# Sums of y squared as rows: nine columns with one column of ones as the weights, and the squares moving

## The chip, the cores and the metric

One core of one Trainium2 chip. The metric is device time in microseconds (us) of one execution of the program; lower is better. TensorE (PE in the rows; its weight loads PEld), VectorE (DVE), ScalarE (ACT), GpSimd (POOL) and SyncE (SP, which issues the DMAs) run side by side and wait for one another by semaphores.

## The reference

One layer of a hybrid decoder step: a feed-forward half step, a mixer of two heads side by side (S5 and SSD), a second half step, a last norm. All is f32; 1024 prompt positions and 8 x 4 sample positions, 1056 in all. What matters here is the end of the SSD head: `y` is divided by the root of its mean square over the 384 channels of its group, for each position and each of four groups.

```python
ys = (ys + ssd_d.astype(f32)[:, None] * xh).reshape(b, l, SSD_WIDTH) * jax.nn.silu(z)
yg = ys.reshape(b, l, SSD_GROUPS, SSD_WIDTH // SSD_GROUPS)
yg = yg * lax.rsqrt(jnp.mean(yg * yg, axis=-1, keepdims=True) + EPS)
o_ssd = yg.reshape(b, l, SSD_WIDTH) * ssd_norm.astype(f32)
out = jnp.concatenate([o5, o_ssd], axis=-1).astype(h.dtype) @ w_out
```

## The kernel before

Channels lie on partitions, positions in the free dimension. Each large product is done in three matmuls of a high and a low part (L317 to L319 in `dense`: weights 128x128, three blocks of 352 positions, four PSUM banks in turn in the mixer). These matmuls are the clock of the program: after each unit of three, `tick` counts one, and other work is put between units. There are two queues of such steps (`later`: a step runs so many ticks after the one before it in its queue), and `at` for a step at a set tick. The order of instructions on each engine is the order in which they are written out this way; nothing reorders them later.

While the projections of SSD group g + 1 run in `dense` (`group`: eight tiles of 24 units each), the chunked scan of group g runs in queue 0 (`ssd_steps`; its sequence is in `steps`). The 1056 positions are nine chunks: c = 0 to 7 of 128 positions, and c = 8, the 32 sample positions, which is done first. For each chunk, `stage_a` makes the decays and transposes (L1744 to L1747), `stage_b` multiplies (L1801 with 64 weight columns, two halves of the array at once; L1802 with 128) and `y_done` makes `y`, its squares over the three channel tiles, and on GpSimd their sum over the three in `ysq` (128 channels x positions). `y_sums` sums `ysq` over its 128 partitions: one f32 matmul (L1787) with `ysq` as the weights and one column of ones moving, which gives one column with positions on partitions, and a VectorE step L1788 (in the rows L152, the helper `ts`) that scales it into column c of `rv` [128, 9]. It is called with the next chunk's `stage_b`, behind L1802, or alone: for c = 6 and c = 8 in `sample_done`, for c = 7 in the tail. In the trace an f32 matmul is two instructions, so the 36 sums are 72.

The last steps of a group are its tail, three steps that run at the start of the next group's sequence, 4, 10 and 5 ticks apart: `stage_b(7)`; the last sum and `rs_root` (a square root on ScalarE, then a reciprocal and eight steps of Newton's method on VectorE, all on [128, 9], L392 to L397); and `rs_row` (L399 to L405): a transpose on TensorE to [9, 128], a VectorE copy of it into `rr`, and the store of that to `rsd[2 + g]` in DRAM. For group 3 the tail runs under the output projection (`mix_out`). From `rsd` it is loaded back, spread over 128 partitions (`rs_load`, L409), when the output projection of the group is prepared (`begin`, `ahead`). `rs_col`, `rs_root` and `rs_row` also serve the three norms over the 1024 channels (`rs_steps`), which the change leaves as they are: of the seven transposes L403, four are the tails'.

`tmp()` hands out three SBUF slices in turn, `abank()` the side banks of PSUM in turn.

Of the kernel before, what the change touches and what calls it, by code (L numbers as in the profile page):

```python
# [31 lines left out]
EPS = 1e-6  # L32
RND = 12582912.0
ADD, SUB, MUL = ALU.add, ALU.subtract, ALU.mult
# [100 lines left out]
class Build:  # L135
# [249 lines left out]
        self.ts(v[0:32, 8:9], ps[0:32, 8:9], 1.0 / n, MUL, EPS, ADD)  # L385
        yield from self.rs_root(y)

    def rs_root(self, y):
        nc, v, t = self.nc, self.rv, self.rt
        self.act(t, v, AF.Sqrt)  # L390
        yield 2
        nc.vector.reciprocal(y, t)  # L392
        for _ in range(2):
            self.tt(t, y, y, MUL)
            self.tt(t, t, v, MUL)
            self.ts(t, t, -0.5, MUL, 1.5, ADD)
            self.tt(y, y, t, MUL)  # L397
# [1287 lines left out]
    def ssd_tiles(self, S):  # L1685
        f = lambda name, *s: S.tile([128, *s], F32, name=name)
        self.abc = f("abc", 6, 128)
        self.ysq = f("ysq", 128)
        self.xb = Slots(S, 3, [128, 5, 128], F32, "xb")
        self.zg = Slots(S, 2, [128, 3, 128], F32, "zg")  # L1690
        self.prod = deque((f(f"dec{i}", 6, 128), f(f"ce{i}", 6, 128), f(f"xd{i}", 384), f(f"xds{i}", 384), f(f"bt{i}", 128))
                          for i in range(2))
        self.hT, self.hS, self.yf = f("hT", 384), f("hS", 384), f("yf", 3, 128)
        self.h0 = Slots(S, 3, [128, 384], F32, "h0")
        self.ces, self.ys, self.xs, self.zs = f("ces", 6, 32), f("ys", 3, 32), f("xsm", 3, 32), f("zsm", 3, 32)
        self.bst = S.tile([96, 128], F32R, name="bst")
        self.bm = [S.tile([96, 128], F32R, name=f"bm{i}") for i in range(2)]
        self.xst = S.tile([96, 384], F32R, name="xst")
        self.tail, self.rs_done = [], set()

    def ssd_steps(self, g):
        nc, L, o = self.nc, self.later, self.o
# [15 lines left out]
        def load_z(c):  # L1718
            n = 32 if c == 8 else 128
            z = self.zs if c == 8 else self.zg.get()  # L1720
            nc.sync.dma_start(z, self.dZ[g, :, :, 128 * c:128 * c + n].rearrange("j p c -> p j c"))
            cur["z", c] = z
# [48 lines left out]
        def y_done(c, n, x, z, p3, s):  # L1771
            cs = slice(128 * c, 128 * c + n)
            y = self.yf[:, :, 0:n]
            for j in range(3):
                self.stt(y[:, j], x[:, j], self.dcol[:, 3 * g + j:3 * g + j + 1], p3[:, j], MUL, ADD)
            self.tt(y, y, z, MUL)
            self.act(s, y, AF.Square)
            self.store(self.dO[g, :, :, cs].rearrange("j p c -> p j c"), y)
            self.tt(s[:, 0], s[:, 0], s[:, 1], ADD, nc.gpsimd)
            self.tt(self.ysq[:, 0:n], s[:, 0], s[:, 2], ADD, nc.gpsimd)  # L1780
            cur["sum"] = (c, n, self.ysq[:, 0:n])

        def y_sums(p):

            if "sum" in cur:
                c, n, s = cur.pop("sum")
                nc.tensor.matmul(p[0:n, 400:401], s, self.ones[:, 0:1], start=True, stop=True)  # L1787
                return lambda: self.ts(self.rv[0:n, c:c + 1], p[0:n, 400:401], 1.0 / 384, MUL, EPS, ADD)  # L1788
            return lambda: None

        def stage_b(c):
            xb, (dec, ce, xd, xds, bt) = cur.pop(c)
            z = cur.pop(("z", c))
            p3, p4 = self.abank(), self.abank()
            for j in range(3):
                for off in range(2 if c else 1):
                    for e in range(2):
                        out = p3[64 * e:64 * e + 64, 128 * j:128 * j + 128]
                        r = 2 * j + e
                        lhs, rhs = ((xd, dec), (self.hT, ce))[off]  # L1800
                        nc.tensor.matmul(out, lhs[:, 64 * r:64 * r + 64], rhs[:, r], start=(off == 0), stop=(off == 1 or c == 0))  # L1801
            nc.tensor.matmul(p4[:, 0:384], bt, xds, start=True, stop=True)  # L1802
            done = y_sums(p3)
            yield GAP["b_pe"]
            done()
            if c == 0:
                nc.vector.tensor_copy(self.hT, p4[:, 0:384])
            else:
                self.tt(self.hT, self.hS, p4[:, 0:384], ADD)
            if c < 7:  # L1810
                self.tt(v6(self.hS), v6(self.hT), self.cd[:, c + 1, h6, None].broadcast_to([128, 6, 64]), MUL, nc.gpsimd)
            yield GAP["b_y"]
            y_done(c, 128, xb[:, 2:5], z, p3[:, 0:384].rearrange("p (j c) -> p j c", j=3), xd.rearrange("p (j c) -> p j c", j=3))
            self.xb.put(xb)
            self.zg.put(z)
            if c == 7:
                nc.sync.dma_start(o["ssdp"][g], self.hT)

        def sample_load(b):
            h0 = self.h0.get()  # L1820
            nc.sync.dma_start(h0, self.a["h0"][g, :, b])
            cur["h", b] = h0
# [9 lines left out]
        def sample_m(b):  # L1832
            self.ts(self.bm[b % 2], self.bst.bitcast(F32), self.bmask[:, b:b + 1], MUL)

        def sample_out(b):
            h0 = cur.pop(("h", b))
            nc.sync.dma_start(o["ssds"][g, :, b], h0)
            self.h0.put(h0)

        def sample_h(b):  # L1840
            h0, bm, p = cur["h", b], self.bm[b % 2], self.abank()
            if b:
                sample_out(b - 1)
            if b + 2 < 8:
                self.at(GAP["sample"], lambda: sample_load(b + 2))
            for r in range(6):
                out = p[64 * (r % 2):64 * (r % 2) + 64, 384 + 4 * (r // 2):388 + 4 * (r // 2)]
                nc.tensor.matmul(out, h0[:, 64 * r:64 * r + 64], self.ces[:, r, 4 * b:4 * b + 4], start=True, stop=True)
            nc.tensor.matmul(p[:, 0:384], bm, self.xst, start=True, stop=True)
            self.tt(v6(h0), v6(h0), self.cds[:, b, h6, None].broadcast_to([128, 6, 64]), MUL, nc.gpsimd)  # L1850

            def add():
                y = self.ys[:, :, 4 * b:4 * b + 4]
                self.tt(y, y, p[:, 384:396].rearrange("p (j c) -> p j c", j=3), ADD)
                self.tt(h0, h0, p[:, 0:384], ADD)
                if b < 7:
                    sample_m(b + 1)

            self.at(GAP["add"], add)

        def sample_done():
            y_sums(self.abank())()
            sample_out(7)
            y_done(8, 32, self.xs, self.zs, self.ys, self.xs)
            nc.vector.memset(self.rv[:, 8:9], 1.0)
            yield GAP["done4" if g == 3 else "done2"]
            y_sums(self.abank())()

# [6 lines left out]
        def steps(nxt=None):  # L1875

            tail, self.tail = self.tail, [
                lambda: stage_b(7),
                lambda: (y_sums(self.abank())(), self.rs_root(self.ry))[1],
                lambda: (self.rs_row(self.ry, self.rsd[2 + g]), self.rs_done.add(g)),  # L1880
            ]
            ga, gb, gh = (GAP[k + ("3" if g == 3 else "")] for k in "abh")
            for i in range(9):
                c = (i + 8) % 9
                L((GAP["first"], GAP["second"])[i] if i < 2 else ga, lambda c=c: stage_a(c))
                if i == 0:
                    for n, fn in enumerate(tail):
                        L(GAP[f"tail{n}"], fn)
                    L(0, lambda: (load_z(8), load_z(0), sample_load(0), sample_load(1), sample_m(0)))
                else:  # L1890
                    L(gb, sample_b if i == 1 else lambda c=c: stage_b(c - 1))
                    if c < 7:
                        L(0, lambda c=c: self.at(6, lambda: load_z(c + 1)))
                    L(gh, lambda b=i - 1: sample_h(b))
            if nxt:
                L(0, nxt)
            L(GAP["done3" if g == 3 else "done"], sample_done)
# [250 lines left out]
```

## Time and profile before

| | |
|---|---|
| median of 3 runs | 2311.99 us (2311.85 to 2312.82) |
| profiled execution | 2316.52 us, of which the span of its instructions is 2314.8 us |
| busy in the span | TensorE 98%, VectorE 65%, ScalarE 37%, GpSimd 16% |
| mean granted TensorE clock | 0.993 |

A row of the time order gives the start in us from the span's start, the duration, engine, line, operation, output<-inputs, the shape of the weights (rows*columns) and the moving operand, the count of merged instructions, and in brackets the idle time ahead of it. A matmul's duration holds its latency; how fast they follow one another is read from the starts. A list of waits gives the total in us, the count and the longest one.

### The profile page before, as it was taken

Reading aid. Unit: us, or ns where it says so; the run is one execution under the profiler, and the core shown is the slowest. Engines: PE = TensorE matmul, PEld = TensorE weight load, DVE = VectorE, ACT = ScalarE, POOL = GpSimd, SP = SyncE. Lnnn points to the kernel's source line nnn. Section 1 sums busy time; section 2 is a strip of 40 time slices with the busy share of each in tenths; the row PEclk is TensorE's granted clock in tenths of the full one; section 3 lists DMA queues with packets and bytes.
Section 4 is the critical chain, followed back from the end, with each engine's and each line's share of the span. In section 5 each row is a group of like instructions: output and inputs, shape, how many; then the busy total and the mean of one; then the engine's idle time right before and its main releaser. Section 6 shows DMA issues by size and latency. Waiting matters only on the chain. (4 is left out here: it accounts for less than half of the span.)

```text
span 2314.8 us, 40918 instructions
## 1 busy us (share of the span) xinstructions
PE 2274.9 (98%) x16463; PEld 2218.2 (96%) x16463; DVE 1503.8 (65%) x3110; ACT 845.0 (37%) x1373; POOL 363.8 (16%) x425
## 2 busy tenths in 40 slices
PE   9999999999999999999999999999999999999997
PEld 9999999999999899999999889999999999999997
DVE  5988887662326377787889778867855555552325
ACT  5433344440113133455555563233433333331122
POOL 1200000000002133242333434422100000000013
PEclk9999999999999999999999999999999999999999
DMA  4222233362311354563555645432222122263112
GB/s 149 82 68 92 102 118 104 120 227 99 102 54 45 115 189 144 157 189 125 174 159 167 213 126 158 141 127 84 88 79 78 71 84 83 88 243 119 62 48 75
DMA packets 191549, 274.68 MB, mean 119 GB/s; under 512 B 31616, under 2 KB 137343, under 8 KB 191359
## 3 DMA queue, kind: packets, MB, share of 16 engines
q1 hardware_dynamic: 190782, 271.54, 35.8%
q8 instruction: 129, 2.11, 0.4%
q14 instruction: 62, 0.50, 0.1%
q10 hardware_dynamic: 576, 0.52, 0.1%
HBM read 195.17 MB, written 76.84 MB: 118 GB/s over the span
## 5 line engine op out<-in xcount | busy, mean ns | idle before, releaser
L317 PE MATMUL b<-xn,ws 128*128 128x352 f32 (+3 forms) x1776 | 589.7, 332 | 2.9 <-DVE x L145 2.2
L318 PE MATMUL b<-xn,ws 128*128 128x352 f32 (+3 forms) x1776 | 575.0, 324 | 2.4 <-DVE xn L155 2.4
L319 PE MATMUL b<-xn,ws 128*128 128x352 f32 (+3 forms) x1776 | 574.4, 323 | 0.0
L317 PEld LDWEIGHTS b<-xn,ws 128*128 128x128 f32 x1776 | 335.7, 189 | 9.4 <-DVE x L145 3.5
L681 PE MATMUL b<-xn,ws 128*128 128x264 f32 x1184 | 338.3, 286 | 5.4 <-ACT g L158 5.4
L318 PEld LDWEIGHTS b<-xn,ws 128*128 128x128 f32 x1776 | 337.5, 190 | 4.0 <-DVE xn L155 3.0
L683 PE MATMUL b<-xn,ws 128*128 128x264 f32 x1184 | 337.5, 285 | 2.3 <-DVE ws L145 2.3
L682 PE MATMUL b<-xn,ws 128*128 128x264 f32 x1184 | 338.3, 286 | 0.0
L319 PEld LDWEIGHTS b<-xn,ws 128*128 128x128 f32 x1776 | 335.8, 189 | 0.0
L158 ACT ACTIVATE ws<-wr 128x512 fp32r<-128x512 f32 (+4 forms) x208 | 170.4, 822 | 328.7 <-PE b L318 271.8
L145 DVE TENSOR_TENSOR ws<-wr,ws 128x512 fp32r<-128x512 f32 (+4 forms) x208 | 220.3, 1060 | 81.5 <-ACT ws L158 81.0
L681 PE MATMUL b<-d,ws 128*128 128x264 f32 x888 | 253.6, 286 | 1.0 <-DVE g L145 0.8
L682 PE MATMUL b<-d,ws 128*128 128x264 f32 x888 | 253.4, 285 | 0.0
L683 PE MATMUL b<-d,ws 128*128 128x264 f32 x888 | 252.3, 284 | 0.0
L155 DVE SCALAR_TENSOR_TENSOR x<-b,x 128x352 f32<-128x352 f32 (+2 forms) x144 | 73.4, 522 | 246.4 <-PE b L319 246.3
L681 PEld LDWEIGHTS b<-xn,ws 128*128 128x128 f32 x1184 | 223.3, 189 | 7.3 <-ACT g L158 6.7
L145 DVE TENSOR_TENSOR g<-b,g 128x264 f32<-128x264 f32 (+1 forms) x311 | 134.2, 433 | 147.5 <-PE b L683 104.5
L683 PEld LDWEIGHTS b<-xn,ws 128*128 128x128 f32 x1184 | 223.8, 189 | 3.1 <-DVE ws L145 3.1
L145 POOL TENSOR_TENSOR acc<-acc,g 128x400 f32<-128x400 f32 (+2 forms) x25 | 37.6, 1505 | 1195.8 <-ACT g L158 1195.6
L682 PEld LDWEIGHTS b<-xn,ws 128*128 128x128 f32 x1184 | 223.2, 189 | 0.0
L317 PE MATMUL b<-d,ws 128*128 128x352 f32 (+2 forms) x534 | 172.7, 323 | 0.0
L319 PE MATMUL b<-d,ws 128*128 128x352 f32 (+2 forms) x534 | 172.1, 322 | 0.0
(344 smaller groups left out, 4255.8 us busy)
## 6 DMA issues: line engine op xcount, KB each, us to landing
wr<-in_gu SPq DMA_DIRECT2D x68, 512.0 KB
dH<-g SPq DMA_DIRECT2D x74, 264.0 KB
wr<-in_win SPq DMA_DIRECT2D x36, 512.0 KB
wr<-in_dn SPq DMA_DIRECT2D x32, 512.0 KB
d<-dH SPq DMA_DIRECT2D x24, 528.0 KB
abc<-dA SPq DMA_DIRECT2D x32, 384.0 KB
xn<-dH SPq DMA_DIRECT2D x20, 528.0 KB
dC<-acc SPq DMA_DIRECT2D x20, 528.0 KB
```

Source lines behind the costliest of these rows:

```text
L145: (eng or self.nc.vector).tensor_tensor(out, x, y, op=op)
L155: self.nc.vector.scalar_tensor_tensor(out, x, s, y, op0=op0, op1=op1)
L158: self.nc.scalar.activation(out, x, f, **k)
L317: nc.tensor.matmul(p, wh[:, kc], xh, start=(k == 0), stop=False)
L318: nc.tensor.matmul(p, wh[:, kc], xl, start=False, stop=False)
L319: nc.tensor.matmul(p, wl[:, kc], xh, start=False, stop=(k == K - 1))
L681: nc.tensor.matmul(q, wh, xh, start=(k == 0 and name in ("P1", "P2", "P5")), stop=False, skip_group_check=True)
L682: nc.tensor.matmul(q, wh, xl, start=False, stop=False, skip_group_check=True)
L683: nc.tensor.matmul(q, wl, xh, start=False, stop=(k == 3), skip_group_check=True)
```

## The change

The sum's operands change places. The weights are nine columns [128, 9] cut from a new tile `hot` of 17 columns, all zeros but the middle one, so that the ones stand in column c of the nine; `ysq` moves. The result has the sums of chunk c in row c of [9, 128] and zeros in the other rows, and VectorE adds it onto `yr` (which is the old `rr` [9, 128]). When all nine are in, `y_root` scales, takes the root as before but on [9, 128], and stores the result itself; the transpose, its copy and the third step of the tail go. The result lies in a slice of `tmp()`, the scratch in `ysq`, and `yr` is cleared for the next group.

```diff
-    def rs_root(self, y):
-        nc, v, t = self.nc, self.rv, self.rt
+    def rs_root(self, y, v=None, t=None):
+        nc, v, t = self.nc, self.rv if v is None else v, self.rt if t is None else t
...
+        self.hot, self.yr = f("hot", 17), self.rr
+        self.nc.vector.memset(self.hot, 0.0)
+        self.nc.vector.memset(self.hot[:, 8:9], 1.0)
+        self.nc.vector.memset(self.yr, 0.0)
...
                 c, n, s = cur.pop("sum")
-                nc.tensor.matmul(p[0:n, 400:401], s, self.ones[:, 0:1], start=True, stop=True)
-                return lambda: self.ts(self.rv[0:n, c:c + 1], p[0:n, 400:401], 1.0 / 384, MUL, EPS, ADD)
+                q = p[0:9, 384:384 + n]
+                nc.tensor.matmul(q, self.hot[:, 8 - c:17 - c], s, start=True, stop=True)
+                return lambda: self.tt(self.yr[:, 0:n], self.yr[:, 0:n], q, ADD)
...
+        def y_root():
+            y_sums(self.abank())()
+            self.ts(self.yr, self.yr, 1.0 / 384, MUL, EPS, ADD)
+            y = self.tmp()[0:9, 0:128]
+            yield from self.rs_root(y, self.yr, self.ysq[0:9])
+            nc.sync.dma_start(self.rsd[2 + g], y)
+            nc.vector.memset(self.yr, 0.0)
...
             y_done(8, 32, self.xs, self.zs, self.ys, self.xs)
-            nc.vector.memset(self.rv[:, 8:9], 1.0)
...
                 lambda: stage_b(7),
-                lambda: (y_sums(self.abank())(), self.rs_root(self.ry))[1],
-                lambda: (self.rs_row(self.ry, self.rsd[2 + g]), self.rs_done.add(g)),
+                y_root,
+                lambda: self.rs_done.add(g),
```

## Rows read from the trace of the kernel before

**Rows 1.** The page, busy time by engine: us, share of the span, instructions.

```profile
PE 2274.9 (98%) x16463; PEld 2218.2 (96%) x16463; DVE 1503.8 (65%) x3110; ACT 845.0 (37%) x1373; POOL 363.8 (16%) x425
```

**Rows 2.** Stretch 940 to 1515: length, busy PE, PEld, DVE, ACT, POOL; clock, DMA.

```profile
940.00:1515.00 575.00, 567.08 (x4212) 533.42 (x4212) 470.82 (x1075) 285.02 (x406) 208.97 (x252) 0.99 0.52 160
```

**Rows 3.** TensorE's waits from 940 to 1620, the two longest groups: total, times, longest.

```profile
PE b L1787 <- POOL ysq L145: 4.2, 2, 3.2
PE b L318 <- DVE xn L155: 2.4, 2, 1.7
```

**Rows 4.** TensorE in order of time: an old sum over 128 positions.

```profile
1064.56 0.32 PE L318 MATMUL b<-xn,ws 128*128 128x352 f32 x1
1064.72 0.32 PE L319 MATMUL b<-xn,ws 128*128 128x352 f32 x1
1064.88 0.28 PE L1787 MATMUL b<-ones,ysq 128*128 128x1 f32 x2
...
1065.27 0.33 PE L318 MATMUL b<-xn,ws 128*128 128x352 f32 x1
```

**Rows 5.** The same view: an f32 matmul with 128 weight and 128 moving columns.

```profile
1094.62 0.38 PE L1744 MATMUL b<-xb 128*128 128x128 f32 x2
1094.83 0.27 PE L1745 MATMUL b<-ident,xb 128*128 128x128 f32 x1
```

**Rows 6.** The same view: the old sum over the 32 sample positions.

```profile
1067.83 0.32 PE L319 MATMUL b<-xn,ws 128*128 128x352 f32 x1
1068.09 0.22 PE L1787 MATMUL b<-ones,ysq 128*32 128x1 f32 x2
1068.24 0.43 PE L317 MATMUL b<-xn,ws 128*128 128x352 f32 x1
1068.51 0.32 PE L318 MATMUL b<-xn,ws 128*128 128x352 f32 x1
```

**Rows 7.** The same view, earlier: into an f32 matmul with 16 weight columns.

```profile
309.69 0.28 PE L682 MATMUL b<-xn,ws 128*128 128x264 f32 x1
309.81 0.28 PE L683 MATMUL b<-xn,ws 128*128 128x264 f32 x1
310.02 0.63 PE L1216 MATMUL b<-x,x 64*16 64x128 f32 x16
```

**Rows 8.** The same view: from 64 weight columns to 128, in a chunk's second stage.

```profile
981.97 0.39 PE L1801 MATMUL b<-ce,hT 128*64 128x128 f32 x4
982.29 0.91 PE L1802 MATMUL b<-xds,bt 128*128 128x384 f32 x2
983.04 0.28 PE L1787 MATMUL b<-ones,ysq 128*128 128x1 f32 x2
```

**Rows 9.** Line L403, weight loads: ns min/median/max, first and last start.

```profile
L403 PEld LDWEIGHTS b<-ident,ry x7: 87/87/133, 46.8 to 1594.6; 128*9 128x9 f32 x7
```

**Rows 10.** TensorE in order of time: transposes in group 0's and group 3's tail.

```profile
1089.79 0.32 PE L319 MATMUL b<-xn,ws 128*128 128x352 f32 x1
1090.18 0.27 PE L403 MATMUL b<-ident,ry 128*9 128x128 f32 x1
...
1090.45 0.32 PE L318 MATMUL b<-xn,ws 128*128 128x352 f32 x1
...
1510.99 0.32 PE L319 MATMUL b<-xn,ws 128*128 128x352 f32 x1
1511.78 0.28 PE L403 MATMUL b<-ident,ry 128*9 128x128 f32 x1 [0.46 <-DVE ry L145]
...
1512.05 0.32 PE L318 MATMUL b<-xn,ws 128*128 128x352 f32 x1
```

**Rows 11.** VectorE groups from 940 to 1515: busy us, mean ns, idle before.

```profile
L152 DVE TENSOR_SCALAR rv<-b 128x1 f32<-128x1 f32 x32 | 4.8, 150 | 1.2 <-PE b L1787 1.1
L145 DVE TENSOR_TENSOR rt<-rt,rv 128x9 f32<-128x9 f32 x8 | 1.4, 171 | 0.3
L404 DVE COPY rr<-b 9x128 f32<-9x128 f32 x4 | 1.1, 276 | 0.5 <-PE b L403 0.5
```

## The prediction

> **What bounds the kernel now.** I read the busy times of the page first. TensorE is busy for 98% of the span, so the reader is to see that whatever lengthens TensorE's stream lengthens the kernel, unless it falls into one of the few places where TensorE waits [rows 1]. The next view is the table of one stretch, from 940 to 1515 us, in which all of the changed code runs: TensorE 567.1 of 575.0 us, VectorE 470.8, the others far less [rows 2]. VectorE has 104 us to spare there, TensorE 8. The third view is the list of TensorE's waits around that stretch: the longest are two waits of the old sums themselves for GpSimd's `ysq`, 4.2 us together, and two for VectorE's `xn`, 2.4 us [rows 3]. All else was read from the order of TensorE's instructions in time, where what counts is the distance between starts, since matmuls are pipelined and a matmul's own duration holds its latency. Undisturbed, two matmuls of 352 columns start 0.16 us apart [rows 4].
>
> **What the change does to TensorE: the sums.** There are 36 of them, nine in each of four groups: eight over 128 positions (c = 0 to 7) and one over 32 (c = 8). Each is one f32 matmul, which the trace shows as two instructions. Before, the squares are the weights (128 columns of them) and one column of ones moves. From the start of the L319 ahead to the start of the L318 behind it takes 0.55 us instead of 2 x 0.16, so an old sum of 128 costs 0.23 us [rows 4]: that is two weight loads, since the moving column is next to nothing. After, the weights are the nine columns cut from `hot`, and the squares move, 128 columns. What 128 moving f32 columns cost is in the L1744 rows: its two instructions take from 1094.62 to 1094.83, 0.105 each, 0.21 together [rows 5]. By that alone old and new would be equal, 0.23 and 0.22.
>
> What decides is another thing in the rows: an f32 matmul whose weights have few columns doesn't run in a stream with the full ones. The old sum of c = 8 has 32 weight columns and one moving column. The L319 ahead of it is followed after 0.26 us instead of 0.16, and from that L319 to the L318 behind it takes 0.68 us, so it costs 0.36 us although it moves and loads less than the old sum of 128 [rows 6]. The pause at the entry, 0.10, stands also before L1216, with 16 weight columns: 0.21 from the L683 ahead, where 0.12 is the rule [rows 7]. At the exit a pause stands behind L1801, whose weights have 64 columns: its last four start 0.32 us ahead of L1802, where their work is 0.22 (two halves at once, so twice the 0.105), and the two full ones of 384 columns that follow take 0.75 where three times 0.21 is 0.63 [rows 5, 8]: 0.10 + 0.12. So the new sum of 128, between full matmuls, is estimated as 0.10 of entry, 0.21 of moving, 0.02 for a first load that wasn't fetched ahead, and 0.22 of exit: 0.55 us. The other way round, the old sum of c = 8, 0.36, plus 0.21 for the columns moved, less some 0.05 for its own two short instructions (0.15 from the first of them to the L317 behind, the exit's 0.10 included), gives 0.52 [rows 6]. I take 0.54, so 0.31 more for each of 32 sums: 9.9 us. The four sums of 32 positions moved one column and now move 32; both pay the pauses; a quarter of 0.21 is 0.05, of which a part is covered: +0.03 each, 0.1 together.
>
> Is nine columns like 16, 32 and 64, or like 128? The nearest row by width speaks for 128: L403, a transpose, has nine weight columns too, loaded in 87 ns [rows 9], and its group 0 row, 1089.79 to 1090.45, has only the L403's own time and a wait in it [rows 10]; in other transposes no entry pause is to be seen. But L403 is a transpose, and L1787 at 32 and L1216 at 16 are plain f32 matmuls as the new one is. I take the nearest in kind. [...]
>
> **TensorE: the transposes.** Four of the seven L403 go. In the last group it is 1510.99 to 1512.05, 1.06 us against 0.32, so 0.74, of which 0.46 is waiting for VectorE's last step of the root; in the first group 0.66 against 0.32, so 0.34 [rows 10]; the two between them, read in the same way, 0.23 and 0.12. Gain: 1.4 us. No wait takes their place on TensorE, since nothing on it reads the root any more; the root's row goes from VectorE straight to the store, and the load of it that the next stage needs stands behind that.
>
> **The other engines.** VectorE: 32 evictions of one column, 150 ns, become adds of 9x128 out of PSUM, which the copy of L404 stands for, 276 ns [rows 11]: with the four small ones 36 x 0.13 = 4.7 us. The root's operations go from 128x9, 171 ns, to 9x128; taken as the same 276 ns, the nine of a root are 0.95 us more, and with the scaling and the clearing that are new, less the copy L404, about 1.1; 4.4 in all [rows 11]. These 9 us lie in VectorE's 104 us of idle time [rows 2]; ten operations of the root stand in one row ahead of evictions, but four PSUM banks turn in the dense loop and each is filled for 24 matmuls, 3.8 us, so a delay of 1 us is covered. If that cover is gone, they are paid in full (a rival below). Three clearing operations at the opening of the pool, under 0.3 us each by the copy's row, stand on VectorE ahead of the first eviction of group 1; `hot` lies where the S5 stage's `un0` was, which was last read by slice 5 of 8, so they wait for nothing recent. ScalarE: one square root of 128 elements for one of nine, four times, off the path. The store of the root moves from the third step of the tail to the second, ahead of what SP issues in those 5 ticks: loads of z and h stood behind it before as well; stores of `acc` can now wait for the end of the root, some 1 us, and are next needed a whole tile (24 units of three matmuls, 11.5 us) later. GpSimd's next write of `ysq` must wait for the root that uses it as scratch, and comes a whole chunk later. The ring of `tmp` turns once more and the ring of side banks once less per group; both have had their readers finished by then. All these I cost at nothing.
>
> **The sum.** 9.9 + 0.1 - 1.4 = 8.6 us. Two of the new sums wait for `ysq` anyway [rows 3], and there the entry pause is hidden: -0.2. So +8.4 us on the profiled execution's 2316.5 us (2314.8 of span and 1.7 around it). Its time is 0.2% over the median of the runs shown, 2312.0, and the stretch is TensorE's in both, so I add it to the median: 2320.4 us. With the spread of the single terms (0.29 to 0.33 for a sum, 1 us for the rest) the case has 2318 to 2323.
>
> **Rivals.** (A) Nine columns run as full ones do, and the nine-column load is cheap: then a new sum is the 0.21 of moving with a little of the next load, against 0.23, and a sum of 32 falls from 0.36 to about 0.15. 32 x -0.01, 4 x -0.2 and -1.4 make -2.5: 2309.5 us, no slower. It decides if a new sum costs under 0.4 us. For it speaks L403, against it L1787 at 32 and L1216. 12%. [...] The trace speaks against it for f32, with 0.105 for each instruction [rows 5]; I leave it 2 of the 12.
>
> (B) The time is absorbed: the 4.2 us for which the sums wait for GpSimd [rows 3] could shrink by as much as TensorE comes later. That takes up to 4.2 us off: 2316. Against it: the work that GpSimd is late with hangs on VectorE and ScalarE steps that are issued by TensorE's own count of units, so it moves along. 8%, 2313 to 2317.
>
> (C) VectorE's 9 us bite: the adds and the roots stand ahead of evictions and of the `xn` that TensorE waits for, or a clearing waits for the old owner of its place. If a third to a half of the 9 us comes through, 2323 to 2326. For it: VectorE is the second busiest, 82% of the stretch [rows 2]; against it, the longest of TensorE's waits for it are two with 2.4 us together [rows 3]. 14%.
>
> **How the numbers follow.** Forecast 66%, A 12, B 8, C 14. The predicted time is the forecast's, 2320.4. The range reaches through B and C, 2313 to 2326, and leaves out A and the far ends. A measurement of this kernel can tell some 0.2%, 4.6 us, from no change: faster than 2307.4 is only the end of A, 3%; between that and 2316.6 lie the rest of A, most of B and a strip of the forecast, 17%; slower 80%.
>
> **What the profile after would show.** Right: behind each L1802 a gap of 0.1 us before the sum; weight loads of nine columns that start with their matmul and not one matmul ahead; 0.5 to 0.55 us from the last full matmul to the next full stream; only three L403; the span longer in the 940 to 1515 stretch alone. Wrong: nine-column loads fetched ahead and no gap (A), more and longer waits of TensorE for VectorE (C), or the waits for `ysq` gone (B).

## The result, and the profile after

The kernel after takes 2328.78 us (median of 6 runs) against 2312.09 for the kernel before in the same series: a ratio of 1.0069, 95% interval 1.0058 to 1.0080, so 16.7 us between the medians and 13 to 18 by the interval. It is slower, as forecast, but by about twice the forecast 8.4 us, and above the top of the range, 2326. The profiled execution took 2327.22 us (span 2325.5, granted clock 0.994).

The first part of the profile's page, busy time by engine, beside [rows 1]: TensorE 6.9 us more, VectorE 10.3 us more, where the prediction had 9.

```profile
span 2325.5 us, 40911 instructions
PE 2281.8 (98%) x16459; PEld 2208.7 (95%) x16459; DVE 1514.1 (65%) x3113; ACT 846.0 (36%) x1373; POOL 367.4 (16%) x425
```

TensorE in order of time, one new sum of 128 positions between full matmuls (columns as in [rows 4]):

```profile
1048.97 0.91 PE L1808 MATMUL b<-xds,bt 128*128 128x384 f32 x2
1049.82 0.39 PE L1793 MATMUL b<-ysq,hot 128*9 128x128 f32 x2
1050.13 0.43 PE L317 MATMUL b<-xn,ws 128*128 128x352 f32 x1
1050.40 0.32 PE L318 MATMUL b<-xn,ws 128*128 128x352 f32 x1
```

The same place before, which continues [rows 8]:

```profile
983.18 0.41 PE L317 MATMUL b<-xn,ws 128*128 128x352 f32 x1
983.42 0.32 PE L318 MATMUL b<-xn,ws 128*128 128x352 f32 x1
```

From the start of the chunk's last full matmul of 384 columns (L1808, before L1802) to the L318 behind the sum it was 982.29 to 983.42, 1.13 us. It is now 1.43. So a new sum costs 0.29 to 0.30 us more; over the 30 of the 32 in whose neighbourhood TensorE doesn't wait, followed to the fourth matmul behind the sum, it is 0.293 in the mean, which makes 9.4 us for 32. The weight loads show how: those of nine columns start with their matmul and not one matmul ahead, and the load of the next L317 comes late too (TensorE's weight loads; idle time in brackets):

```profile
1049.82 0.10 PEld L1793 LDWEIGHTS b<-ysq,hot 128*9 128x9 f32 x2 [0.55 <-issue]
1050.13 0.19 PEld L317 LDWEIGHTS b<-xn,ws 128*128 128x128 f32 x1 [0.22 <-issue]
```

The rest of the lost time stands in TensorE's waits, 940 to 1630 us (total, times, longest), beside [rows 3]:

```profile
PE b L317 <- DVE x L145: 6.0, 4, 2.7
PE b L1793 <- POOL ysq L145: 3.2, 1, 3.2
PE b L318 <- DVE xn L155: 2.1, 2, 1.4
PE b L1808 <- DVE h L145: 1.6, 2, 0.8
PE b L317 <- ACT tb L158: 0.7, 1, 0.7
```

The same list of before has 2.2 us for `x`, 0.8 for `h` and no row for `tb`. Four places make the difference. In order of time, before has only the third of them, with 0.72 us:

```profile
1272.93 0.91 PE L1808 MATMUL b<-xds,bt 128*128 128x384 f32 x2 [0.74 <-DVE h L145]
...
1397.94 0.44 PE L317 MATMUL b<-xn,ws 128*128 128x384 f32 x1 [0.67 <-ACT tb L158]
...
1409.95 0.40 PE L317 MATMUL b<-xn,ws 128*128 128x288 f32 x1 [1.84 <-DVE x L145]
...
1539.17 0.43 PE L317 MATMUL b<-xn,ws 128*128 128x352 f32 x1 [2.69 <-DVE x L145]
```

Together they are 5.94 us, 5.2 more than before. The stage (from the first L1749, before L1744, to the last L381) has grown from 643.5 to 657.1 us, so 13.6: 9.4 of sums, -1.4 of transposes, and 5.2 of these waits are 13.2. Behind these waits stands a longer root. Here is the one of the last group, on VectorE:

```profile
1517.07 0.28 DVE L145 TENSOR_TENSOR rr<-rr,b 9x128 f32<-9x128 f32 x1 [0.76 <-PE b L1793]
1517.38 0.22 DVE L152 TENSOR_SCALAR rr<-rr 9x128 f32<-9x128 f32 x1
1517.75 0.52 DVE L145 TENSOR_TENSOR x<-x,b 128x352 f32<-128x352 f32 x1 [0.16 <-PE b L319]
1519.31 0.94 DVE L392 RECIPROCAL tb<-ysq 9x128 f32<-9x128 f32 x1 [1.04 <-ACT ysq L158]
...
1522.61 0.17 DVE L1873 MEMSET rr<- 9x128 f32 x1
1522.70 1.30 DVE L145 TENSOR_TENSOR x<-x,b 128x352 f32<-128x352 f32 x3
```

The reciprocal takes 0.94 us (it was 0.21 on 128x9), and ahead of it VectorE, in the order of the program, stands idle for 1.04 us until ScalarE has the square root. In the four roots it idles 0.6, 1.3, 1.7 and 1.0 us there; before it was 0.3 in one and nothing in the others. When the row is done three evictions (`x`, 128x352) are queued behind it. Before, two rows of the same view were:

```profile
1509.87 0.21 DVE L392 RECIPROCAL ry<-rt 128x9 f32<-128x9 f32 x1
...
1511.63 0.52 DVE L145 TENSOR_TENSOR x<-x,b 128x352 f32<-128x352 f32 x1
```

From the last sum's arrival to the first eviction behind the root VectorE took 2.8 us then (from 1508.84) and takes 5.6 now, so 2.8 more. What ScalarE does in that time, after and then before (the page's columns, idle time in brackets):

```profile
1517.67 1.28 ACT L158 ACT_TABLE_LOAD   x1 [3.27 <-DVE rr L152]
1518.97 0.31 ACT L158 ACTIVATE ysq<-rr 9x128 f32<-9x128 f32 x1
```

```profile
1506.43 1.28 ACT L158 ACT_TABLE_LOAD   x1
1509.03 0.21 ACT L158 ACTIVATE rt<-rv 128x9 f32<-128x9 f32 x1 [1.31 <-DVE rv L152]
```

Before, the table of the square root was loaded while ScalarE waited for the sums; now the load begins when they are there. The load takes 1.28 us in both. From the last sum's arrival on VectorE to the store of the row it was 3.6 us (1508.84 to 1512.40); it is 5.6 now too. SP, which issues that store, shows the second thing:

```profile
1522.66 0.29 SPq L1872 DMA_DIRECT2D rsd<-tb  x1
1523.05 0.34 SPq L256 DMA_DIRECT2D wr<-in_wos  x1
1523.93 0.32 SPq L409 DMA_DIRECT2D rs<-rsd  x1
1524.35 0.37 SPq L1924 DMA_DIRECT2D raw<-dO  x1
```

```profile
1507.12 0.33 SPq L256 DMA_DIRECT2D wr<-in_wos  x1
1512.40 0.29 SPq L405 DMA_DIRECT2D rsd<-rr  x1
1513.67 0.32 SPq L409 DMA_DIRECT2D rs<-rsd  x1
```

Before (the second fence), a weight load `wr` was issued 5.3 us ahead of the store. Now the store stands ahead of it in the queue, and the load goes out behind it, between the store and the loads of `rs` and `raw`.

The last of the four waits hangs on those loads. GpSimd, ScalarE and VectorE in the kernel after, and GpSimd in the kernel before:

```profile
1531.81 2.47 POOL L145 TENSOR_TENSOR raw<-raw,rs 128x1056 f32<-128x1056 f32 x1 [15.86 <-DMA raw<-dO]
1534.31 1.18 ACT L158 ACTIVATE xn<-raw,wn 128x1056 fp32r<-128x1056 f32 x1 [4.26 <-POOL raw L145]
1535.52 2.29 DVE L155 SCALAR_TENSOR_TENSOR xn<-raw,wn,xn 128x1056 fp32r<-128x1056 f32 x1 [4.24 <-ACT xn L158]
```

```profile
1519.63 2.47 POOL L145 TENSOR_TENSOR raw<-raw,rs 128x1056 f32<-128x1056 f32 x1 [11.69 <-DMA raw<-dO]
```

GpSimd multiplies by the row that came back 9.2 us behind the store's issue, where it was 7.2 before. VectorE stands for 4.24 us at its next step of that chain, with the evictions that TensorE waits for behind it. So at this place VectorE is not short of time; it idles, in order, for a row that comes late.

### The profile page after: what moved, and what is told of

Its sections match the earlier page's. It is cut to its first block, busy times and chain, and to the rows that moved or that the text cites. A ratio compares the mean times of both kernels' runs of the same rounds, so it can differ in the third digit from the quotient of the medians.

```text
span 2325.5 us, 40911 instructions
## 1 busy us (share of the span) xinstructions
PE 2281.8 (98%) x16459; PEld 2208.7 (95%) x16459; DVE 1514.1 (65%) x3113; ACT 846.0 (36%) x1373; POOL 367.4 (16%) x425
## 4 chain that ended last, share of the span: by engine, by line
PE 83%; DVE 8%; DMA 4%; ACT 2%; issue 2%; POOL 1%; SPq 0%; DVEq 0%; ACTq 0%; POOLq 0%
PE b L317 15%; PE b L319 14%; PE b L318 14%; PE b L681 9%; PE b L682 9%; PE b L683 9%; DVE x L145 2%; PE b L1807 2%; PE b L346 1%; PE b L347 1%; PE b L348 1%; DVE ws L145 1%; PE b L1808 1%; DVE g L145 1%; DVE xn L145 1%
## 5 line engine op out<-in xcount | busy, mean ns | idle before, releaser
L317 PE MATMUL b<-xn,ws 128*128 128x352 f32 (+3 forms) x1776 | 589.4, 332 | 7.6 <-DVE x L145 6.0
L318 PE MATMUL b<-xn,ws 128*128 128x352 f32 (+3 forms) x1776 | 574.2, 323 | 2.1 <-DVE xn L155 2.1
L317 PEld LDWEIGHTS b<-xn,ws 128*128 128x128 f32 x1776 | 334.9, 189 | 21.5 <-issue 8.7
L318 PEld LDWEIGHTS b<-xn,ws 128*128 128x128 f32 x1776 | 336.7, 190 | 3.7 <-DVE xn L155 2.7
L317 PE MATMUL b<-d,ws 128*128 128x352 f32 (+2 forms) x534 | 172.6, 323 | 0.0
```

The costliest lines, as they stand in the source:

```text
L317: nc.tensor.matmul(p, wh[:, kc], xh, start=(k == 0), stop=False)
L318: nc.tensor.matmul(p, wh[:, kc], xl, start=False, stop=False)
```

## The experiments

Two theories were to be told apart. By the theory of the weights, the narrow weights of the sums cost TensorE its stream, and that is all. By the theory of the root, its longer way over VectorE, ScalarE and SP comes through in waits besides. Ratios are against the kernel before in the same series, with 95% intervals; a stage is the one defined above, 643.5 us in before. Stages and waits are those of the one execution that was profiled, which in some runs lay over 4 us above the run's median.

**Width of the weights.** `hot` becomes 80 or 72 columns wide and a sum takes 72 or 64 of them; the rows of the result beyond the nine are not read.

```diff
-        self.hot, self.yr = f("hot", 17), self.rr
+        self.hot, self.yr = f("hot", 80), self.rr
...
-                nc.tensor.matmul(q, self.hot[:, 8 - c:17 - c], s, start=True, stop=True)
+                nc.tensor.matmul(p[0:72, 384:384 + n], self.hot[:, 8 - c:80 - c], s, start=True, stop=True)
```

(64: `f("hot", 72)`, `p[0:64, ...]`, `8 - c:72 - c`.)

> The changed kernel with 72 weight columns instead of nine (the rest are zeros; rows 9 to 71 of the result are not read). Array theory (few weight columns put TensorE's array into another arrangement, with a pause at both ends, 0.29 us per sum): no gap of 0.09 us ahead of a sum, a sum costs 0.22 to 0.24 us, and the kernel is 8.5 to 10 us faster than the changed one. Rival, the moving of 128 columns itself or the later steps cost the time: within 2 us of the changed kernel. By the array theory some 4 to 7 us over the kernel before are left, for the root and its store.

> The same with 64 weight columns, only eight fewer than the 72. Array theory with the limit at 64, as the 64-column matmuls of the second stage show it: the pauses stay, 0.5 us per sum, within 1.5 us of the changed kernel. Rival, the cost falls with the number of columns: the time lies at that of the 72 columns.

Measured: 72 columns 2323.59 us, 1.0044 (1.0030 to 1.0058); 64 columns 2331.62, 1.0080 (1.0066 to 1.0093). TensorE in order of time, 72 first, then 64:

```profile
979.76 0.91 PE L1808 MATMUL b<-xds,bt 128*128 128x384 f32 x2
980.51 0.38 PE L1793 MATMUL b<-ysq,hot 128*72 128x128 f32 x2
980.65 0.41 PE L317 MATMUL b<-xn,ws 128*128 128x352 f32 x1
980.90 0.32 PE L318 MATMUL b<-xn,ws 128*128 128x352 f32 x1
```

```profile
981.08 0.91 PE L1808 MATMUL b<-xds,bt 128*128 128x384 f32 x2
981.92 0.43 PE L1793 MATMUL b<-ysq,hot 128*64 128x128 f32 x2
982.28 0.43 PE L317 MATMUL b<-xn,ws 128*128 128x352 f32 x1
982.55 0.32 PE L318 MATMUL b<-xn,ws 128*128 128x352 f32 x1
```

1.14 us with 72 columns, the old sum's 1.13; 1.47 with 64. Eight columns more in the weights take 0.33 us off a sum. That settles what the sums cost: the pauses are the narrow weights' and go with them. The time with 64 is 4.2 us over the kernel after (2327.47, below), where at most 1.5 was expected; by the sums, 0.34 us each for 0.29, it is 1.5, and the medians leave over 4 us of uncertainty. The price of the 64 columns, by the starts in the two fences, is 0.09 us in (0.84 less 0.75) and 0.22 out (0.36 less 0.14). What the array does in these pauses no row shows: that it takes another arrangement, as in the array theory of the expectations, was a supposition, and so was a limit at 64 exactly, since no width between 64 and 72 was tried. But as the whole cause the weights fall: without the pauses the kernel still takes 10 us more than before, and the 8.5 to 10 us that were expected back did not come. Its waits at the four places are 1.34, 1.06, 1.84 and 2.38 us, at the first two longer than in the kernel after: where TensorE is sooner, it waits longer for an engine that isn't. So by the medians only 3.9 us of the sums' 9.4 came back here (2327.47, below, less 2323.59, uncertain by over 4), and in the stage 6.2 (657.1 less 650.9).

> The changed kernel once more, beside the kernel before on this chip: a ratio of 1.006 to 1.008, with a wait of 2 to 3 us for VectorE's x behind the last root if that is of the kernel and not of one execution; waits that come and go elsewhere show how far one execution stands for the median.

Measured: the kernel after in the same series, 2327.47 us, 1.0060 (1.0046 to 1.0074); stage 660.4, waits at the four places 5.88 us.

**The store in its old place.** The root's row is stored in the tail's third step again.

```diff
-            nc.sync.dma_start(self.rsd[2 + g], y)
...
+            cur["root"] = y
...
-                lambda: self.rs_done.add(g),
+                lambda: (nc.sync.dma_start(self.rsd[2 + g], cur.pop("root")), self.rs_done.add(g)),
```

> The changed kernel with the store of the root issued in the third step of the tail, where the kernel before had it, so that the weight load stands ahead of it on SP again. Queue theory: in the last group the weight load is issued some 7 us earlier than in the changed kernel, the wait of 2.7 us for VectorE's x near 1536 shrinks to 1 us or less, and the kernel is 2 to 4 us faster. Rival, the root itself is late (reciprocal 0.94 us, table load behind the wait): the wait stays, within 1 us of the changed kernel.

Measured: 2324.10 us, 1.0043 (1.0030 to 1.0057), 3.4 less than the kernel after in its series, with intervals that overlap; so what this run shows is read from its trace. The weight load is issued at 1516.93, 7.6 us ahead of the store. GpSimd's product follows the store, issued at 1524.48, by 7.1 us again:

```profile
1531.58 2.47 POOL L145 TENSOR_TENSOR raw<-raw,rs 128x1056 f32<-128x1056 f32 x1 [13.82 <-DMA raw<-dO]
```

VectorE's wait at its step of the chain falls from 4.24 to 2.23, and of TensorE's four waits only the last changes, from 2.69 to 0.69: the moved store is what made most of that one, by the weight load that it let in ahead of `rs` and `raw`.

**The table ahead of the wait.** `y_root` begins with a square root of a column of ones into `rt`, which isn't used.

```diff
         def y_root():
+            self.act(self.rt[:, 0:1], self.ones[:, 0:1], AF.Sqrt)
             y_sums(self.abank())()
```

> The changed kernel with one more step at the head of the root: ScalarE takes the square root of one column of ones, which nothing reads, so that the table load of 1.28 us stands ahead of the wait for the sums and not behind it. Theory of the late root (VectorE's order is held up by the root): the reciprocal starts 1.2 us earlier behind the scaling, VectorE's wait for ScalarE in a root falls from 1.0 to 1.7 us to 0.4 or less, the store goes out 1.2 us earlier, and the kernel is 2 to 4 us faster than the changed one. Rival, only the arrangement of the array and the place of the store count: within 1 us of it.

Measured: 2324.21 us, 1.0040 (1.0025 to 1.0055). The first two of the four waits are gone, the third is 1.55, the last 1.85. The time lies 3.3 us under the kernel after's 2327.47, which the noise of the two medians could make alone; the waits are the evidence.

**A longer root in the kernel before.** The old root, and behind each of the four tail roots three reciprocals of 9x128 that change nothing that is used, 2.8 us of VectorE; sums, transposes and table as before, and the store in its old place, though its row is ready later.

```diff
+        def long_root():
+            yield from self.rs_root(self.ry)
+            for _ in range(3):
+                nc.vector.reciprocal(self.rr, self.rr)
...
-                lambda: (y_sums(self.abank())(), self.rs_root(self.ry))[1],
+                lambda: (y_sums(self.abank())(), long_root())[1],
```

> The kernel before, with three reciprocals of 9x128 (0.94 us each, of a tile that is overwritten afterwards) behind each root on VectorE: 2.8 us more in each of the four tails, nothing else changed. Theory of the late VectorE: the waits that the changed kernel has and the kernel before has not (0.8 near 1271, 1 to 2 at 1393 to 1404, 2 to 3 at 1528) appear here, 3 to 6 us in all. Rival, VectorE's 104 us of idle time cover it: under 1 us.

Measured: 2318.07 us, 1.0020 (1.0010 to 1.0030), so 4.6 us by the interval's middle; stage +5.8. TensorE in order of time, its waits at the four places:

```profile
1268.82 0.91 PE L1802 MATMUL b<-xds,bt 128*128 128x384 f32 x2 [0.59 <-DVE h L145]
...
1392.56 0.44 PE L317 MATMUL b<-xn,ws 128*128 128x384 f32 x1 [0.92 <-ACT tb L158]
...
1404.62 0.40 PE L317 MATMUL b<-xn,ws 128*128 128x288 f32 x1 [1.90 <-DVE x L145]
...
1531.83 0.43 PE L317 MATMUL b<-xn,ws 128*128 128x352 f32 x1 [0.96 <-DVE x L145]
```

The same four waits, in a kernel in which nothing else of the change is. A longer root on VectorE is enough to make them; it is longer here by the same 2.8 us as the last root of the change. The last one is 0.96 and not 2.69, with the weight load ahead of the store as before.

**Table and store with 72 columns.** Each alone, and both together.

> 72 weight columns and the early table load, with the store of the root left where the change put it. With 72 columns alone the stretch from 945 to 1640 takes 7.6 us more than in the kernel before, with table and store together 0.9 us less. If the late root is what takes most of that, 4 to 6 us of the 8.5 go by the table alone, since VectorE is later than TensorE in the third and fourth group only because it idles in the root. Rival, the store: 2 us or less go, and the wait of 2 to 3 us behind the last root stays.

> 72 weight columns and the store in the third step, with the table load left behind the wait. If the store's place is worth 2 to 3 us, in the last group alone, that much goes and the waits near 1271 and from 1393 to 1404 stay as with 72 columns alone. Rival, the store holds up SP in every group and with it the loads on which VectorE's steps wait: 4 us or more go.

> 72 weight columns, the early table load and the store in the third step together. If the three causes add up (array 5 to 9 us, store 2 to 4, table 2 to 4), 3 us or less over the kernel before are left, and what is left stands as waits for VectorE at its late places (near 1271, 1393 to 1404, 1528 of the kernel before). Rival, the longer root by itself (reciprocal 0.94 us, eight steps at 0.28) keeps VectorE late: 4 to 7 us over.

| 72 columns, and | us | ratio | stage | waits at the four places, us |
|---|---|---|---|---|
| nothing | 2323.59 | 1.0044 (1.0030 to 1.0058) | +7.4 | 1.34, 1.06, 1.84, 2.38 |
| the store in third place | 2317.99 | 1.0021 (1.0012 to 1.0030) | +5.8 | 1.33, 1.02, 1.85, 1.06 |
| the table early | 2315.37 | 1.0010 (1.0000 to 1.0019) | +1.4 | 0.17, 0, 1.86, 0.77 |
| both | 2314.92 | 1.0004 (0.9994 to 1.0014) | -1.0 | 0.17, 0, 1.87, 0 |

The table is what the first two waits hang on, and it alone takes 6 us off the stage; the last one hangs on both, and the third on neither. For the store alone the run is not clear: its waits fall as expected, by 1.3 us in the last group alone, and the stage by 1.6, but the medians by 5.6, which is what the rival asked for (4 or more); the profiled execution lay 4.7 us above its median. With both the kernel is level with the one before. VectorE and ScalarE then, last root:

```profile
1506.67 0.22 DVE L152 TENSOR_SCALAR rr<-rr 9x128 f32<-9x128 f32 x1
1507.33 0.94 DVE L392 RECIPROCAL tb<-ysq 9x128 f32<-9x128 f32 x1
```

```profile
1503.81 1.28 ACT L158 ACT_TABLE_LOAD   x1
1505.11 0.20 ACT L158 ACTIVATE rt<-ones 128x1 f32<-128x1 f32 x1
1506.98 0.31 ACT L158 ACTIVATE ysq<-rr 9x128 f32<-9x128 f32 x1 [1.67 <-DVE rr L152]
```

The reciprocal starts 0.66 us behind the scaling, where it was 1.93 in the kernel after. By the medians the early table is worth 3.3 us at nine columns and 8.2 at 72, the width 3.9 with the late table and 8.8 with the early one; each of these is uncertain by 4 us or more, so that the two savings don't simply add up is not shown by the times. The four waits point that way: the early table takes 2.5 us off them at nine columns and 3.8 at 72.

**A shorter root.** On top of both, ScalarE's reciprocal square root takes the place of root and reciprocal (in the early step too), and two Newton steps of three instructions that of two of four.

```diff
-            self.act(self.rt[:, 0:1], self.ones[:, 0:1], AF.Sqrt)
+            self.act(self.rt[:, 0:1], self.ones[:, 0:1], AF.Abs_reciprocal_sqrt)
...
-            yield from self.rs_root(y, self.yr, self.ysq[0:9])
+            v, t = self.yr, self.ysq[0:9]
+            self.act(y, v, AF.Abs_reciprocal_sqrt)
+            yield 2
+            for _ in range(2):
+                self.tt(t, y, y, MUL)
+                self.stt(t, t, -0.5, v, MUL, MUL)
+                self.stt(y, t, 1.5, y, ADD, MUL)
```

> The same with a short root: ScalarE gives 1/root by its own function, and VectorE's two Newton steps are six operations of 9x128 instead of a reciprocal and eight, some 1.9 us in place of 3.6. If VectorE's time in the root is what was left, its waits go back to those of the kernel before, and with the transposes gone the kernel is 0 to 3 us faster than the kernel before. If the 36 longer additions are to blame (36 x 0.12 us), 2 to 4 us over it stay.

Measured: 2311.03 us, 0.9989 (0.9980 to 0.9999), 2.5 us under the kernel before by the ratio, and the only one here that beats it, barely. Of the four waits one is left, the third, 0.58 us where it was 1.87: that one hangs on the root's length on VectorE. So a kernel with the change can be had at a small gain, when its sums are wide, its table early, its root short and its store late. The short root was not tried in the kernel before, so whose gain that is, the change's or the short root's, stays open.

## Why the prediction was wrong in its size

**The sums: right.** Forecast +0.31 us each, measured +0.293; 9.9 against 9.4 us. The choice between L403, a transpose with nine columns, and L1216 and L1787, plain matmuls with 16 and 32, fell on the right side, and rival A, that nine columns run as full ones do, falls by the 0.29 us; the 2 of its 12% that it has for a sum shorter still rest on nothing that a run shows. A new sum costs 0.52 us in all, forecast 0.54: 0.10 at the entry as forecast and 0.21 of moving leave 0.21 behind it, for which 0.22 of exit and 0.02 of a late first load were taken. No row shows the 0.02 by itself. The small sums of 32 positions cost what they did, 0.35 us, where 0.03 more was expected.

**The transposes: right.** 1.4 us forecast, and 1.4 gained. Between the same two matmuls, with and without the transpose, TensorE gains 0.35 us at the first of the four and 0.74 at the last, against 0.34 and 0.74.

**"All these I cost at nothing": this is the step that failed.** Four waits of TensorE, 5.2 us more of them in the stage, came of what was priced at nothing, and three of its terms were wrong. The nine operations of the root were all priced by a copy of 9x128, 276 ns; that is right for the adds (269) and products (280) and wrong for the reciprocal, 941: 0.66 us more in every root. The square root was "off the path", but VectorE waits for it, and the table load, which had stood ahead of the wait for the sums, stood behind it: 1.0 us of idling in the last root. So the last root held VectorE up 2.8 us more, where 1.1 was priced and called covered. And the store was moved "ahead of what SP issues in those 5 ticks", for which the prediction names loads of z and h and stores of `acc`; it left out the weight load `wr`, which the order of SP's issues shows 5.3 us ahead of the old store. That load now stood between the store and the loads that wait for it, and the row came back 2 us later still.

**The cover was judged by the wrong number.** 104 us of idle time in the stretch [rows 2] and four banks of 3.8 us say that a delay of 1 us is covered; the delay was 2.8 us in the last root, and VectorE's steps stand in the order of the program, so that what it was late with came back as waits at later places where TensorE is close behind it, the four above, of 0.67 to 2.69 us. From the second root to the first of the four waits, 1229 to 1273 in the kernel after, VectorE is busy for 41.1 of 44 us: the idle time of the whole stretch is not to be had where it is needed. That places exist where TensorE is close behind was to be read: [rows 3] has two waits for `xn`, and the same list, further down, had 2.2 us for `x`.

**Rival C was the nearest, and had half of it.** It was given 14% and a third to a half of VectorE's 9 us, so 2323 to 2326. Its roots that stand ahead of evictions are what the longer root in the kernel before shows (4.6 us). But it has no term for the table load on ScalarE and none for the store on SP, and with the table loaded early and the store late (72 columns) no loss clear of the noise is left (1.0004), though the 36 longer adds, which C named too, are still there. Measured, beyond sums and transposes: 11.6 us with the sums' pauses taken out (72 columns: 10.2, plus 1.4 of transposes), and between 6 and 8 beside them (15.9, the ratio's middle, less 9.4, plus 1.4 is 7.9; in the stage of the kernel after 5.6). Rival B, absorption, is seen in part: the first wait for `ysq` is gone in the kernel after's profile (4.2 us became 3.2), but stands in its second one, with 4.4.

**What stays open.** Why the table load fell behind the wait isn't shown: the square root's operands and its output changed at the same time, and no run took them apart. The four waits, the sums and the transposes close the account of a stage within 1.1 us in the kernel after and in four of the ten runs above; in the other six 2 to 4 us more are lost. Much of that is TensorE's clock: in these six the granted clock stands at 0.5 for 10.2 to 13.7 us of the stage, where the kernel before has 6.8 (the four have 3.4 to 10.2, the kernel after 10.2); half of the time beyond that, 1.7 to 3.4 us, is the estimate of what it costs at most, since at 0.50 two matmuls of 352 columns start 0.29 us apart instead of 0.16 (before, 1316.4 to 1318.8). In the kernel before it falls behind two waits of TensorE, of 1.70 us at 1315.5 and 3.17 at 1345.5, but it doesn't fall behind each: with 72 columns and the store in third place it is 0.50 from 1408.5 to 1411.5, behind the third wait of 1.85 us, with matmuls of 288 columns 0.24 us apart, and with 72 columns alone it stays at 1.00 behind the same wait of 1.84, with 0.13 us. So that wait of 1.85 us cost more than its length: by these distances about 1.4 us more, an estimate. The clearing of `hot` and `yr` at the opening of the pool was not tried by itself; its three operations take 0.3 us at 939.4 in the kernel after, and TensorE doesn't wait in the 20 us behind them.

## What to carry to other kernels

Price a step that changes its shape operation by operation, by rows of that operation and that count of elements a partition: here a step moved from 128 partitions of 9 elements to 9 of 128 did the same work in more time, and its reciprocal in over four times as much. Where a step lies between two others on three engines, follow its chain from its last input to its last reader, table loads included, and list everything that each queue issues between its old place and its new one; the idle time of an engine over a stage doesn't tell whether a delay of 3 us is made good before the next reader. And of a narrow f32 matmul in a stream of full ones, look at the weights' columns first: padding them with zeros from nine to 72 took a sum from 1.43 us back to 1.14 here, where the old one had 1.13.

## What the runs showed of the hardware

- Between full f32 matmuls, a sum with 64 weight columns costs 0.33 us more than one with 72 (1.47 against 1.14 us between the same neighbours), though it loads less.
- VectorE's reciprocal took 941 ns on 9x128 and 215 on 128x9, where a product took 280 and 171: the same 1152 elements took longer with more of them in a partition, and the reciprocal's time rose the more of the two.
- With a weight load issued between a small store and the loads that bring it back, the row of the last group was used 8.3 to 9.4 us behind its store (six traces); with the weight load ahead of the store, 7.0 to 7.3 us (the six others).
- Behind the same wait of TensorE, 1.84 and 1.85 us, the granted clock stayed at 1.00 in one execution (72 columns alone) and fell to 0.50 in another (72 columns, store in third place); matmuls of 288 columns followed one another after 0.13 and 0.24 us.
- The table load of the square root, 1.28 us, stood ahead of the wait for its input in the kernel before and behind it in the kernel after. A square root that needs nothing, placed first, brought it ahead again: the load began at 1503.81 and the square root of the sums at 1506.98 (72 columns, table and store).
